# Attention block: MLA scores placed among v's products, value products among r's, weight splits for v and w_out on ScalarE and VectorE

## The chip, the cores and the metric

The kernel runs on one core of one Trainium2 chip. The metric is the device time of one execution in microseconds (us). The core has a tensor engine (PE for its products, PEld for its weight loads), a vector engine (DVE), a scalar engine (ACT), GpSimd (POOL) and SyncE (SP), whose queue issues nearly all transfers from HBM. Each engine works through its own instruction list in order. They wait for one another through semaphores.

## The reference, cut to what matters

The program computes two transformer blocks on 256 tokens of width 1024. The first block adds 16 meta tokens in front, projects the normed input `u` with `w_in`, runs a gated linear attention (GLA) and a latent softmax attention (MLA) side by side, joins them through `w_out`, and then runs a mixture of 64 experts. The second block (convolution and mLSTM mixers with feed-forward layers) follows and is not touched.

```python
z = u @ w_in                                   # q, k, v, r, a_low, q_lat, kv_lat, k_rope
y_gla = gla_group(q, k, v, r, a_low, ...)      # chunks of 64, 4 heads, gate silu(r) at the end
y_mla = mla_group(q_lat, kv_lat, k_rope, ...)  # scores, masked softmax, p @ v, 4 heads of 128
h = h + concat([y_gla, y_mla]) @ w_out
h = h + hier_moe(rmsnorm(h), ...)              # top 2 of 64 experts, 6.3 MB of weights each
```

All tensors are float32. Where the change works, weights and activations are split into a high part (fp32r, a rounded copy) and a low part (the rest), and a product is summed from three passes: high x high, high x low, low x high.

## The kernel before

`phase_a` holds the whole attention block. It streams `w_in` in 1 MB pieces and forms, in this order, the small latent projections (tiles `z`), q and k of GLA (`z` again), v (`v`, lines 671 to 680) and r (`r`, lines 690 to 707), and then the products with `w_out` (`wo`, lines 709 to 732). Every weight piece is split by `split` (line 1100): ACT writes the high part `wh`, and DVE, or POOL where the call has `gp` set, subtracts it from the raw piece and writes the low part `wl` (line 1120). The calls with `gp` are the first piece of the small projections, both pieces of v (line 675) and piece 3 of `w_out` (line 714). The tiles of high and low parts come from a pool of four buffers, so two pieces are alive at a time.

The order on PE is the order in which the Python code records it, with one addition. Side work is written as generators (`gates`, `keys`, `queries`, `values`, `gla`, `attend(b)` for the two blocks b of 128 queries). Each `yield` names a cost. A `unit` of main products advances a clock by its own cost and then `poll` runs every generator that has come due. So what a generator records lands on PE between two units. The other engines' lists are sorted by a scheduler that keeps the dependencies.

`attend(b)` forms the scores of four heads (tiles `qo`, `kn`, `qr_bd`, `kr`), takes the row maximum on DVE and the exponential on ACT into `pr`, transposes `pr` into `pT`, multiplies with the values `va` (the value products, line 508), divides by the sum, transposes again and splits the result into `yT`. `gla` does the same for the linear attention: transposes of `edl`, masked `attm`, the states `S`, the output products (`ps<-v,attm` and `ps<-S,q_bd`), the norm, the gate with `rg` and the split into `yT`.

At the start the input is normed: ACT and DVE form the row scale, DVE writes `x`, PE transposes it, ACT and DVE write the high and low parts `uT` (lines 290 to 312).

The weights of `w_out`, of the memory projection (`wkv`), the memory itself (`mem`) and the experts (`eg`, `eu`, `ed`, 1 MB pieces, six for each expert) go through a ring of buffers. SP issues a load when the buffer that it takes is free and the loads ahead of it in SP's list are issued. Seven more buffers appear where the attention's own tiles were (`a_done`, line 746), five more where `uT` and the split tiles were, after the last `wo` product. After `w_out` come the router (`route`, `router`), the gather of tokens and the experts.

Of the kernel before, what the change touches and what calls it, by code (L numbers as in the profile page):

```python
# [10 lines left out]
F32 = mybir.dt.float32  # L11
F32R = mybir.dt.float32r
# [77 lines left out]
class Kern:  # L90
# [150 lines left out]
    def phase_a(self):  # L241
# [71 lines left out]
        nc.gpsimd.memset(self.mv, 1.0)  # L313
# [144 lines left out]
        def y_tiles():  # L458
            if not yT:
                yT.extend(pw.tile([P, 2, KD, P], F32R, tag=f"uT{q}", name=f"yT{q}") for q in range(2))  # L460
            return yT

        def o_tile():
            if not late:
                late.append(self.mp.tile([P, 4, 4, P], F32, tag="xs", name="late"))
            return late[0]

# [5 lines left out]
        def attend(b, *needs):  # L473
            for c in needs:
                self.finish(c)
# [19 lines left out]
            yield 3.5  # L495
            pT = self.hl.tile([P, 2048], F32, tag="hl", name=f"pT{b}")[:, :1536].rearrange("p (j g t) -> p j g t", j=3, g=4)
            for j in range(2 + b):
                c0, n = toks[j]
                p = self.ps()
                pv = p.rearrange("p (a b) -> p a b", b=P)  # L500
                for g in range(4):
                    self.T(pv[:n, g, :], pp[:, g, c0:c0 + n])
                (nc.vector.tensor_copy if j != 1 else nc.scalar.copy)(pT[:n, j], pv[:n])
            yield 2.5
            ym = o_tile()[:, b]
            for g2 in range(2):
                p = self.ps()
                pv = p[:, :258].rearrange("p (a b) -> p a b", b=129)
                for gg in range(2):
                    for j in range(2 + b):  # L510
                        n = toks[j][1]
                        self.mm(pv[:, gg, :], pT[:n, j, 2 * g2 + gg, :], va[:n, j, 2 * g2 + gg, :],
                                start=j == 0, stop=j == 1 + b)
# [3 lines left out]
            yield 2.5  # L517
# [4 lines left out]
            self.split_t(*(t[:, b, 4:8] for t in y_tiles()), pv)  # L522

        def gla():
# [30 lines left out]
            yield 1.5  # L555
            self.finish(vc)
# [38 lines left out]
            for b in range(2):  # L595
                ov, o[b] = o[b], o_tile()[:, 2 + b]
                nc.vector.tensor_tensor(o[b], ov, self.bc(ri[:, b, :], [P, 4, P]), ALU.mult)
            past.append("o")
            yield 5.0
# [5 lines left out]
            for b in range(2):  # L605
# [6 lines left out]
                self.split_t(*(t[:, b, 0:4] for t in y_tiles()), yt)  # L612
# [61 lines left out]
        vf = [sb.tile([P, NT], F32, tag=f"rw{q}", name=f"vf{q}") for q in "oxtk"]  # L674
        for hf in range(2):
# [14 lines left out]
        self.finish(gt)  # L690
        attm = t4([P, 2, 4, P], "attm")
        kdt = sb.tile([NM, 2, P], F32, tag="qt", name="kdt")
        nc.gpsimd.memset(attm, 0.0)
        rp = [self.ps("r") for _ in range(2)]
        rdone = []
        ac = [None, None]
        vc = self.chain(values())
        oc = self.chain(gla())
        for hf in range(2):
            ws = self.split(rw[hf])  # L700
            for b in range(2):
                tpart(rp[b], ws, hf, 1 + b)
                if hf == 0:
                    ac[b] = self.chain(attend(b, kc, qc))
# [7 lines left out]
        for q, b in ((2, 0), (2, 1), (3, 0), (3, 1), (0, 0), (1, 0), (0, 1), (1, 1)):  # L712
            if q not in ws:
                ws[q] = self.split(wo[q], q == 3)
            self.wait(oc if q < 2 else ac[b])
            if not done:
                self.until(lambda: len(past) == 3)
# [4 lines left out]
            hi, lo = ws[q]  # L722

            def go():
                for nh in range(2):
                    cs = slice(nh * 512, nh * 512 + 512)
                    for k in range(2):
                        self.mm3(acc[b][nh], [t[:, b, 2 * q + k] for t in yT], (hi[:, k, cs], lo[:, k, cs]),
                                 q == 2 and k == 0, q == 1 and k == 1)
            self.unit(2.6, go)  # L730
# [5 lines left out]
    def load_memory(self):  # L736

        nc, mp = self.nc, self.mp
        mem = [mp.tile([P, 4 * NT], F32, tag="y", bufs=2, name=f"mem{b}")[:, :D] for b in range(2)]
# [24 lines left out]
    def route(self, b, acc):  # L764
# [8 lines left out]
        yield (1.4, 1.0)[b]  # L773
# [317 lines left out]
    def pair(self, ctx):  # L1091
# [5 lines left out]
        return pool  # L1097

# [807 lines left out]
```

## Time and profile before

| | |
|---|---|
| median of 3 runs | 2136.28 us (2135.34 to 2137.08) |
| profiled execution | 2137.44 us |
| its span, first to last instruction | 2135.7 us |
| mean granted TensorE clock | 0.983 of full |
| PE busy | 1979.5 us (93%) |
| DVE busy | 956.3 us (45%) |
| ACT busy | 665.1 us (31%) |
| POOL busy | 31.3 us (1%) |
| DMA | 605.14 MB, mean 283 GB/s |

The page's second part cuts the span in 40 slices of 53.4 us. The attention block fills the first three slices and part of the fourth (PE busy in tenths 8, 9, 8, 8; PEclk 9, 9, 7, 9; the DMA engines 6, 4, 4, 8). The experts fill the slices up to 21, with the DMA engines at 9 and 413 to 423 GB/s in nearly all of them. The second block fills the rest.

In a timeline row stand the start, the time that the row covers, the engine, the line, the operation, output<-inputs, the partitions x elements and the count, and in brackets the idle time of that engine just before and what ended it. A windows row gives the stretch, its length, the busy time and the count of instructions of PE, PEld, DVE, ACT and POOL, the granted clock (1.00 is 2.4 GHz, 0.50 is 1.2 GHz), the busy share of the DMA engines and GB/s.

### The profile page before, as it was taken

Reading aid. Unit: us, or ns where it says so; the run is one execution under the profiler, and the core shown is the slowest. Engines: PE = TensorE matmul, PEld = TensorE weight load, DVE = VectorE, ACT = ScalarE, POOL = GpSimd, SP = SyncE. Lnnn points to the kernel's source line nnn. Section 1 sums busy time; section 2 is a strip of 40 time slices with the busy share of each in tenths; the row PEclk is TensorE's granted clock in tenths of the full one; section 3 lists DMA queues with packets and bytes.
Section 4 is the critical chain, followed back from the end, with each engine's and each line's share of the span. In section 5 each row is a group of like instructions: output and inputs, shape, how many; then the busy total and the mean of one; then the engine's idle time right before and its main releaser. Section 6 shows DMA issues by size and latency. Waiting matters only on the chain.

```text
span 2135.7 us, 39455 instructions
## 1 busy us (share of the span) xinstructions
PE 1979.5 (93%) x17351; PEld 1454.0 (68%) x17351; DVE 956.3 (45%) x1452; ACT 665.1 (31%) x877; POOL 31.3 (1%) x28
## 2 busy tenths in 40 slices
PE   8989888888889888888889999999999999999998
PEld 7767454444445443544447998879998998888997
DVE  6553322222222222222227545775547445887545
ACT  6423111111111111111114433544434432854432
POOL 3000000000000000000000000000000000000000
PEclk9979999999999999999999999999999999999999
DMA  6448999999999999999995654546555553445551
GB/s 228 177 178 331 420 375 422 421 422 421 422 422 421 422 421 422 421 422 423 413 386 223 237 182 145 206 146 219 188 190 186 196 180 112 145 159 183 192 183 74
DMA packets 86001, 605.14 MB, mean 283 GB/s; under 512 B 9889, under 2 KB 10145, under 8 KB 14914
## 3 DMA queue, kind: packets, MB, share of 16 engines
q1 hardware_dynamic: 85602, 602.55, 71.2%
q8 instruction: 138, 2.26, 0.4%
q14 instruction: 37, 0.30, 0.0%
q10 hardware_dynamic: 224, 0.03, 0.0%
HBM read 601.49 MB, written 1.05 MB: 282 GB/s over the span
## 4 chain that ended last, share of the span: by engine, by line
PE 62%; DMA 28%; DVE 6%; ACT 2%; issue 1%; SPq 0%; DVEq 0%; ACTq 0%
DMA ed<-in_expert_w_down 14%; PE fu L118 11%; PE fd L118 11%; PE fg L118 11%; DMA eu<-in_expert_w_up 9%; DMA eg<-in_expert_w_gate 5%; PE ps L118 4%; PE pd L118 4%; PE po L118 4%; PE cu L118 3%; PE mu L118 2%; PE pg L118 2%; PE mo L118 2%; PE pu L118 2%; DVE wl L1120 1%
## 5 line engine op out<-in xcount | busy, mean ns | idle before, releaser
L973 DVE SCALAR_TENSOR_TENSOR h<-po,G,h 128x512 f32<-128x512 f32 x256 | 192.1, 751 | 354.4 <-PE po L118 334.1
L1120 DVE TENSOR_TENSOR wl<-wc,wh 128x2048 fp32r<-128x2048 f32 (+2 forms) x108 | 240.4, 2232 | 157.2 <-ACT wh L1114 157.1
L1114 ACT ACTIVATE wh<-wc 128x2048 fp32r<-128x2048 f32 (+2 forms) x114 | 213.3, 1872 | 261.3 <-issue 146.9
L118 PE MATMUL pd<-ed,hT 128*32 128x512 f32 x1024 | 244.8, 630 | 40.2 <-DMA ed<-in_expert_w_down 27.3
L118 PE MATMUL po<-y,C 128*128 128x512 f32 x512 | 236.7, 605 | 3.8 <-ACT C L967 3.8
L118 PE MATMUL fd<-wh,hT 128*128 128x512 f32 x704 | 225.5, 396 | 0.0
L118 PE MATMUL fg<-xT,wh 128*128 128x256 f32 x1152 | 203.8, 279 | 0.0
L118 PE MATMUL fu<-xT,wh 128*128 128x256 f32 x1152 | 203.6, 279 | 0.0
L118 PEld LDWEIGHTS po<-y,C 128*128 128x128 f32 x512 | 91.8, 189 | 144.6 <-ACT y L962 72.6
L118 PEld LDWEIGHTS fg<-xT,wh 128*128 128x128 f32 x1152 | 176.8, 188 | 1.7
L118 PEld LDWEIGHTS fu<-xT,wh 128*128 128x128 f32 x1152 | 175.4, 188 | 0.0
L1120 DVE TENSOR_TENSOR wl<-wr,wh 128x2048 fp32r<-128x2048 f32 x52 | 119.1, 2292 | 110.1 <-ACT wh L1114 110.1
L118 PE MATMUL pu<-eu,xg 128*32 128x128 f32 x4096 | 130.7, 274 | 38.2 <-DMA eu<-in_expert_w_up 35.8
L118 PE MATMUL fg<-xT,wl 128*128 128x256 f32 x576 | 160.8, 279 | 0.0
L118 PE MATMUL fu<-xT,wl 128*128 128x256 f32 x576 | 160.8, 279 | 0.0
L947 DVE TENSOR_TENSOR hg<-sg,pu 128x128 f32<-128x128 f32 x64 | 18.4, 288 | 305.3 <-PE pu L118 305.3
L118 PEld LDWEIGHTS fd<-wh,hT 128*128 128x128 f32 x704 | 132.1, 188 | 31.5
L118 PEld LDWEIGHTS pd<-ed,hT 128*32 128x32 f32 x1024 | 50.4, 112 | 142.8 <-issue 91.8
L118 PEld LDWEIGHTS pu<-eu,xg 128*32 128x32 f32 x4096 | 110.0, 110 | 52.0 <-DMA eu<-in_expert_w_up 41.7
L1114 ACT ACTIVATE wh<-wr 128x2048 fp32r<-128x2048 f32 x52 | 99.6, 1917 | 135.9 <-issue 58.5
L118 PE MATMUL fd<-wl,hT 128*128 128x512 f32 x352 | 138.5, 393 | 0.0
L118 PEld LDWEIGHTS pg<-eg,xg 128*32 128x32 f32 x4096 | 107.7, 110 | 44.6 <-issue 38.9
(507 smaller groups left out, 2517.1 us busy)
## 6 DMA issues: line engine op xcount, KB each, us to landing
eg<-in_expert_w_gate SPq DMA_DIRECT2D x128, 1024.0 KB, 19.7
eu<-in_expert_w_up SPq DMA_DIRECT2D x128, 1024.0 KB, 19.7
ed<-in_expert_w_down SPq DMA_DIRECT2D x128, 1024.0 KB, 19.7
wc<-in_ffn_w_gate SPq DMA_DIRECT2D x44, 1024.0 KB, 4.7
wc<-in_ffn_w_up SPq DMA_DIRECT2D x44, 1024.0 KB, 4.6
wr<-in_ffn_w_down SPq DMA_DIRECT2D x44, 1024.0 KB, 4.6
wc<-in_w_in_conv SPq DMA_DIRECT2D x10, 1024.0 KB, 4.7
wr<-in_w_out SPq DMA_DIRECT2D x8, 1024.0 KB, 4.8
```

The lines of the kernel that those rows point to most:

```text
L118: self.nc.tensor.matmul(out, lhsT, rhs, start=start, stop=stop, **kw)
L947: nc.vector.tensor_mul(hg, sg, pu[:, :P])
L973: nc.vector.scalar_tensor_tensor(self.h[:, b, cs], p, self.G[:, b, e:e + 1], self.h[:, b, cs], ALU.mult, ALU.add)
L1114: nc.scalar.activation(hi, raw, AF.Copy)
L1120: (nc.gpsimd if gp else nc.vector).tensor_sub(lo, raw, hi.bitcast(F32))
```

## The change

Nothing is added to or taken from the arithmetic. Eight things differ.

1. `attend` no longer forces its inputs to be complete; it yields until they are. Both `attend` generators and `gla` are started inside v's loop, so the scores stand between v's products of the second half.
2. `attend` waits until both blocks have their scores, then transposes and forms the value products in smaller steps. `r`'s products are recorded in units of one k tile (cost 0.65) and no longer of four (2.6), so the pieces stand between them.
3. Tiles: the transposed probabilities lie in tiles of the block's own pool and, for the 16 meta tokens, in `mv`; the divided result lies in `mk`; MLA's split result has its own tiles `yM` (tag `y`), and `yT` holds GLA's half alone. `mv` is set to one later, by `load_memory`.
4. v, r and `w_out` are split by a new function `split2`: two halves, high part on ACT, low part on DVE, none on POOL.
5. `w_out`'s units are halved, and pieces 0 and 1 (GLA's) are taken together for each half of the columns. The ring grows (`a_done`) once the value products and GLA's output are recorded.
6. `kdt` has a tile of its own.
7. `route` of block 1 yields 0.4 and no longer 1.0.
8. The set-to-one of `mv` at the program's start is gone, so POOL's list begins with `kra`.

```diff
-        nc.gpsimd.memset(self.mv, 1.0)
...
+        def y_mla():
+            if not yM:
+                yM.extend(self.mp.tile([P, 4 * NT], F32R, tag="y", bufs=2, name=f"yM{q}")[:, :1024].rearrange(
+                    "p (b k t) -> p b k t", b=2, k=4) for q in range(2))
+            return yM
...
         def attend(b, *needs):
             for c in needs:
-                self.finish(c)
+                while not c.done:
+                    yield 0.5
...
-            yield 3.5
-            pT = self.hl.tile([P, 2048], F32, tag="hl", name=f"pT{b}")[:, :1536].rearrange("p (j g t) -> p j g t", j=3, g=4)
+            yield 3.0
+            while len(past) < 2:
+                yield 0.5
+            px = t4([P, 1 + b, 4, P], f"pT{b}")
+            pT = [pm[:, b]] + [px[:, j] for j in range(1 + b)]
...
-            yield 1.5
-            self.finish(vc)
+            while not (vc and vc[0].done and len(past) >= 2):
+                yield 0.5
...
-            def go():
-                for k in range(4):
-                    x = [t[:, 4 * hf + k, c0:c0 + n] for t in uT]
-                    self.mm3(dst[:n, :], x, (hi[:, k, :], lo[:, k, :]), hf == 0 and k == 0, hf == 1 and k == 3)
-            self.unit(2.6, go)
+            for k in range(4):
+                x = [t[:, 4 * hf + k, c0:c0 + n] for t in uT]
+                self.unit(0.65, lambda: self.mm3(dst[:n, :], x, (hi[:, k, :], lo[:, k, :]), hf == 0 and k == 0, hf == 1 and k == 3))
...
         for hf in range(2):
-            ws = self.split(vw[hf], True)
+            ws = self.split2(vw[hf])
             for f in range(4):
                 zpart(vp[f][:, :NT], ws, hf, f * P, P, 0)
                 if hf == 1:
                     nc.scalar.copy(vf[f], vp[f][:, :NT])
+                elif f < 2:
+                    ac[f] = self.chain(attend(f, kc, qc))
+                elif f == 2:
+                    oc = self.chain(gla())
...
-        for q, b in ((2, 0), (2, 1), (3, 0), (3, 1), (0, 0), (1, 0), (0, 1), (1, 1)):
-            if q not in ws:
-                ws[q] = self.split(wo[q], q == 3)
-            self.wait(oc if q < 2 else ac[b])
+        for group, b in (((2,), 0), ((2,), 1), ((3,), 0), ((3,), 1), ((0, 1), 0), ((0, 1), 1)):
+            for q in group:
+                if q not in ws:
+                    ws[q] = self.split2(wo[q])
+                self.wait(oc if q < 2 else ac[b])
             if not done:
-                self.until(lambda: len(past) == 3)
+                self.until(lambda: len(past) == 5)
...
+    def split2(self, raw):
+
+        self.n += 1
+        k, n = raw.shape[1:]
+        hi, lo = (self.hl.tile([P, 2048], F32R, tag="hl", name=f"w{q}{self.n}")[:, :k * n].rearrange("p (k n) -> p k n", n=n)
+                  for q in "hl")
+        for u in range(2):
+            ks = slice(u * k // 2, (u + 1) * k // 2)
+            self.nc.scalar.activation(hi[:, ks], raw[:, ks], AF.Copy)
+            self.nc.vector.tensor_sub(lo[:, ks], raw[:, ks], hi[:, ks].bitcast(F32))
+        return hi, lo
```

On PE, the value products (`ps<-va,...`) stood in one piece behind the transposes of `pr` (names: `pT` the transposed probabilities, `late` the result tile).

```order
L115 MATMUL ps_1019<-cst_63,pr_232 16x128 x4
L115 MATMUL ps_1025<-cst_63,pr_232 128x128 x4
L115 MATMUL ps_1031<-cst_63,pr_232 128x128 x4
L118 MATMUL ps_1039<-va,pT_1005 128x129 x4
L118 MATMUL ps_1047<-va,pT_1005 128x129 x4
L118 MATMUL ps_1055<-va,pT_1018 128x129 x6
L118 MATMUL ps_1065<-va,pT_1018 128x129 x6
L115 MATMUL ps_1075<-cst_63,late 128x128 x4
```

Now the first of them stand between products of r's second half.

```order
L118 MATMUL r_840<-wh_951,uT_120 128x512
L118 MATMUL r_840<-wl_952,uT_120 128x512
L118 MATMUL r_840<-wh_951,uT_121 128x512
L118 MATMUL ps_963<-va,mv 128x129
L118 MATMUL ps_963<-va,pT_881 128x129
L118 MATMUL ps_963<-va,mv 128x129
L118 MATMUL ps_963<-va,pT_881 128x129
L118 MATMUL r_840<-wh_951,uT_120 128x512
L118 MATMUL r_840<-wl_952,uT_120 128x512
L118 MATMUL r_840<-wh_951,uT_121 128x512
```

Twelve r products (four units) now follow the last value product, where before nothing of r was left.

On ACT, the end of r and the start of `w_out` before (`yT` both halves of the split result, `wh_1161` piece 3 of `w_out`):

```order
L503 COPY pT_1005<-ps_1012 128x512
L491 ACTIVATE pr_232<-ps_996,mx_999 64x208
L491 ACTIVATE pr_232<-ps_996,mx_999 64x272
L503 COPY pT_1018<-ps_1025 128x512
L1114 ACTIVATE wh_1161<-wo_942 128x2048
L1132 ACTIVATE yT_1081<-rg 128x512
L1132 ACTIVATE yT_1081<-ps_1093 128x512
```

And now (`wh_1172` is piece 3, in the buffer of r's second piece; `yM` MLA's split result; L721 the gate silu(r)):

```order
L608 ACTIVATE rg<-ps_985 128x512
L608 ACTIVATE rg<-ps_1001 128x512
L721 ACT_TABLE_LOAD
L721 ACTIVATE rg<-r_840 128x512
L1125 ACTIVATE wh_1172<-wo_1083 128x1024
L1162 ACTIVATE yM_1071<-ps_1066 128x512
L721 ACTIVATE rg<-r_841 128x512
L1125 ACTIVATE wh_1172<-wo_1083 128x1024
L1162 ACTIVATE yM_1071<-ps_1125 128x512
```

A half of piece 3 now stands ahead of each part of `yM` that the first `wo` products read.

At the program's start the scheduler also put one ACT instruction elsewhere. Before (`wh_239` is the high part of the first small projection, whose low part is POOL's; `uT` the transposed input):

```order
L304 ACTIVATE gx<-gx,ur_129 16x1024
L1132 ACTIVATE uT_120<-ps_172 128x4x128
L1132 ACTIVATE uT_120<-ps_179 128x4x128
L1132 ACTIVATE uT_120<-ps_186 128x4x16
L1132 ACTIVATE uT_120<-ps_193 128x4x16
L1114 ACTIVATE wh_239<-win_100 128x1856
L1132 ACTIVATE uT_120<-ps_200 128x4x128
```

And now:

```order
L304 ACTIVATE gx<-gx,ur_129 16x1024
L1144 ACTIVATE wh_238<-win_100 128x1856
L1162 ACTIVATE uT_120<-ps_172 128x4x128
L1162 ACTIVATE uT_120<-ps_179 128x4x128
L1162 ACTIVATE uT_120<-ps_186 128x4x16
L1162 ACTIVATE uT_120<-ps_193 128x4x16
L1162 ACTIVATE uT_120<-ps_200 128x4x128
```

The weight copy moved from behind four `uT` copies to ahead of all of them.

## Rows read from the trace of the kernel before

**Rows 1.** The page's part 4, the chain that ended last, by engine.

```profile
PE 62%; DMA 28%; DVE 6%; ACT 2%; issue 1%; SPq 0%; DVEq 0%; ACTq 0%
```

**Rows 2.** Windows just before the first expert and through the experts.

```profile
176.00:180.00 4.00, 4.00 (x73) 3.98 (x76) 0.29 (x2) 3.04 (x8) 0.00 (x0) 1.00 0.01 4
...
300.00:1100.00 800.00, 700.93 (x8477) 363.31 (x8475) 201.42 (x338) 120.97 (x263) 0.00 (x0) 0.98 1.01 420
```

**Rows 3.** Timeline of SP and PE: a load behind w_out, the first expert.

```profile
160.45 0.33 SPq L141 DMA_DIRECT2D ed<-in_expert_w_down  x1
...
178.74 1.96 PE L118 MATMUL pg<-eg,xg 128*32 128x128 f32 x64
```

**Rows 4.** Windows of the attention block, cut where PE waits or its clock changes.

```profile
53.35:57.79 4.44, 0.21 (x1) 0.00 (x0) 4.36 (x4) 0.42 (x2) 3.22 (x1) 0.83 0.78 258
57.79:63.03 5.24, 5.24 (x19) 4.83 (x20) 2.42 (x6) 0.85 (x3) 0.00 (x0) 0.50 0.46 181
...
76.12:108.70 32.58, 32.24 (x183) 24.76 (x181) 20.61 (x49) 18.94 (x29) 0.00 (x0) 1.00 0.45 175
108.70:110.76 2.06, 0.00 (x1) 0.00 (x0) 1.83 (x11) 1.21 (x3) 0.00 (x0) 1.00 0.61 207
110.76:112.73 1.97, 1.97 (x10) 1.64 (x10) 1.23 (x5) 0.59 (x1) 0.00 (x0) 0.53 1.02 412
112.73:125.92 13.19, 13.19 (x41) 9.80 (x41) 4.59 (x11) 1.91 (x1) 0.00 (x0) 0.50 0.58 225
125.92:129.06 3.14, 2.46 (x13) 2.22 (x12) 2.21 (x5) 1.27 (x3) 2.71 (x1) 0.68 0.00 0
129.06:132.09 3.03, 0.73 (x3) 0.30 (x3) 3.03 (x3) 0.47 (x1) 1.83 (x1) 0.88 0.00 0
132.09:138.26 6.17, 5.49 (x14) 4.01 (x14) 0.56 (x2) 0.60 (x1) 0.00 (x0) 0.51 0.75 275
...
149.95:151.16 1.21, 0.00 (x1) 0.00 (x0) 1.16 (x1) 0.00 (x0) 0.00 (x0) 1.00 0.02 7
```

**Rows 5.** Timeline of POOL and DVE where both subtract.

```profile
46.57 2.89 DVE L532 TENSOR_TENSOR edl<-zk,edl 128x544 f32<-128x544 f32 x1 [2.11 <-ACT zk L656]
...
52.07 4.50 POOL L1120 TENSOR_TENSOR wl<-win,wh 128x2048 fp32r<-128x2048 f32 x1 [2.30 <-ACT wh L1114]
...
52.25 5.03 DVE L448 TENSOR_TENSOR qr_bd<-qx,qt 64x256 f32<-64x256 f32 x2
...
59.85 0.85 DVE L448 TENSOR_TENSOR qr_bd<-qx,qt 64x256 f32<-64x256 f32 x2
...
128.56 2.88 DVE L1133 TENSOR_TENSOR yT<-rg,yT 128x512 fp32r<-128x512 f32 x1
```

**Rows 6.** Timeline of the program's start: POOL, DVE, SP, ACT, PE.

```profile
4.83 2.34 POOL L290 TENSOR_TENSOR gx<-met,gx 16x1024 f32<-16x1024 f32 x1
...
5.18 1.99 DVE L163 SCALAR_TENSOR_TENSOR u2nt<-ur,um 16x1 f32<-16x1 f32 x1
...
10.28 0.33 SPq L761 DMA_DIRECT2D br<-in_br  x1
...
13.63 1.74 ACT L1114 ACTIVATE wh<-win 128x1856 fp32r<-128x1856 f32 x1
...
15.91 5.35 PE L118 MATMUL z<-uT,wh 128*80 128x272 f32 x32 [0.54 <-ACT uT L1132]
```

**Rows 7.** Timeline of ACT and DVE: prices of steps around w_out.

```profile
100.23 1.28 ACT L491 ACT_TABLE_LOAD   x1 [0.72 <-DVE mx L488]
...
131.36 0.68 DVE L1133 TENSOR_TENSOR yT<-ps,yT 128x512 fp32r<-128x512 f32 x1
...
137.61 0.60 ACT L1132 ACTIVATE yT<-ps 128x512 fp32r<-128x512 f32 x1 [8.08 <-PE ps L115]
...
141.37 1.92 ACT L1114 ACTIVATE wh<-wo 128x2048 fp32r<-128x2048 f32 x1 [3.16 <-PE wo L118]
...
143.32 2.29 DVE L1120 TENSOR_TENSOR wl<-wo,wh 128x2048 fp32r<-128x2048 f32 x1 [4.39 <-ACT wh L1114]
```

More of the change, by code (lines that the diff above doesn't have):

```diff
@@ L456, in phase_a, with y_gla @@
         yT = []
-        def y_tiles():
+        yM = []
+        def y_mla():
[3 more added lines that the diff above has]
+            return yM
+        def y_gla():
             if not yT:
-                yT.extend(pw.tile([P, 2, KD, P], F32R, tag=f"uT{q}", name=f"yT{q}") for q in range(2))
+                yT.extend(pw.tile([P, 2, 4, P], F32R, tag=f"uT{q}", name=f"yT{q}") for q in range(2))
             return yT
@@ L464, in o_tile @@
             if not late:
-                late.append(self.mp.tile([P, 4, 4, P], F32, tag="xs", name="late"))
+                late.append(self.mp.tile([P, 2, 4, P], F32, tag="xs", name="late"))
             return late[0]
+        pm = self.mv.rearrange("p l m h d -> p (l m h d)")[:NM, :1024].rearrange("p (b g t) -> p b g t", b=2, g=4)
+        yo = self.mk.rearrange("p b j m -> p b (j m)").rearrange("p b (g t) -> p b g t", t=P)
         def r_tile():
@@ L502, in attend @@
                     self.T(pv[:n, g, :], pp[:, g, c0:c0 + n])
-                (nc.vector.tensor_copy if j != 1 else nc.scalar.copy)(pT[:n, j], pv[:n])
-            yield 2.5
-            ym = o_tile()[:, b]
+                (nc.vector.tensor_copy if j != 1 else nc.scalar.copy)(pT[j], pv[:n])
+                yield 0.5
+            yield 1.5
+            ym = yo[:, b]
             for g2 in range(2):
@@ L516, in attend @@
                 nc.vector.tensor_tensor(ym[:, 2 * g2:2 * g2 + 2, :], pv[:, :, 0:P], rc.to_broadcast([P, 2, P]), ALU.mult)
-            yield 2.5
+                yield 0.5
+            past.append(f"v{b}")
+            yield 2.0
             p = self.ps()
@@ L521, in attend @@
                 self.T(pv[:, g, :], ym[:, g, :])
-            self.split_t(*(t[:, b, 4:8] for t in y_tiles()), pv)
+            self.split_t(*(t[:, b] for t in y_mla()), pv)
         def gla():
@@ L611, in gla @@
                 nc.vector.tensor_tensor(yt, pv, self.bc(self.col("gla"), [P, 4, P]), ALU.mult)
-                self.split_t(*(t[:, b, 0:4] for t in y_tiles()), yt)
+                self.split_t(*(t[:, b] for t in y_gla()), yt)
         groups = (("kra", 384, 80, 0), ("kv", 256, 128, 0), ("l0", 0, 128, NM), ("l1", 128, 128, NM))
@@ L674, in phase_a @@
         vf = [sb.tile([P, NT], F32, tag=f"rw{q}", name=f"vf{q}") for q in "oxtk"]
+        vc, rdone, ac = [], [], [None, None]
+        self.finish(gt)
+        attm = t4([P, 2, 4, P], "attm")
+        kdt = sb.tile([NM, 2, P], F32, name="kdt")
+        nc.gpsimd.memset(attm, 0.0)
         for hf in range(2):
-            ws = self.split(vw[hf], True)
+            ws = self.split2(vw[hf])
             for f in range(4):
@@ L689, in values @@
                 yield 0.5
[L690 to L693, printed above, removed]
+        vc.append(self.chain(values()))
         rp = [self.ps("r") for _ in range(2)]
[L695 to L698, printed above, removed]
         for hf in range(2):
-            ws = self.split(rw[hf])
+            ws = self.split2(rw[hf])
             for b in range(2):
                 tpart(rp[b], ws, hf, 1 + b)
-                if hf == 0:
-                    ac[b] = self.chain(attend(b, kc, qc))
         for b in range(2):
@@ L721, in phase_a, with go @@
                 acc[b] = [self.ps("wo") for _ in range(2)]
[L722 to L730, printed above, removed]
+            def go(q, nh):
+                hi, lo = ws[q]
+                cs = slice(nh * 512, nh * 512 + 512)
+                for k in range(2):
+                    x = [t[:, b, 2 * q + k] for t in y_gla()] if q < 2 else [t[:, b, 2 * q + k - 4] for t in y_mla()]
+                    self.mm3(acc[b][nh], x, (hi[:, k, cs], lo[:, k, cs]), q == 2 and k == 0, q == 1 and k == 1)
+            for nh in range(2):
+                for q in group:
+                    self.unit(1.3, lambda: go(q, nh))
             if q == 1:
```

10 lines of the change are left out of this document (6 added, 4 removed).

## The prediction

> **What bounds the kernel now.** I read the chain first, then the windows around the hand-over to the experts, then the attention block's windows, and only then single instructions. The chain [rows 1] is PE for 62% and DMA for 28%. The DMA part is the experts' stage: between 300 and 1100 us the DMA engines are fully busy at 420 GB/s [rows 2], and its bytes are fixed. A faster attention block cannot shorten that stage; it can only let it begin earlier. So the question is what starts it. Just before the first expert product at 178.74 [rows 3] the DMA engines stand still (share 0.01 from 176 to 180 [rows 2]): all buffers of the ring are full, and the next load waits until the first expert has used one. The loads before that wait for the attention block too: the load at 160.45 [rows 3] takes a buffer that the last `wo` product frees. Both hand-overs are released by PE, so time that PE gains before 160 us should move the whole experts' stage, one for one.
>
> Within the attention block the reader is to look at two columns of rows 4, PE busy and the clock. PE loses time there in two ways. It stands still: 4.23 us of 4.44 up to 57.79, 0.34 in the long stretch up to 108.70, then 2.06, 0.68, 2.30, 0.68 and 1.21. And it runs at 1.2 GHz instead of 2.4 after the first wait (5.24 us) and, with one short break, from 110.76 to 138.26. The rest of the block runs at full clock without gaps.
>
> **The change part by part.** v's split first. A subtraction on POOL takes 4.50 us, and a DVE instruction with two SBUF inputs that meets it takes until POOL's end: a pair of `qr_bd` additions took 5.03 us beside 0.85 for the same pair later, and `edl` took 2.89 [rows 5]. The first of these holds back the query rows on PE, which is the wait of 4.23; the low clock follows it (5.24 us at 0.50, so 2.62 us lost). *The Trainium skill, "SBUF — State Buffer", section "Who interferes with whom", says that a DVE instruction with two SBUF inputs and a GpSimd instruction that reads SBUF exclude one another for the whole instruction, whoever starts first. These rows agree; what it says against this change stands under the rivals.* With `split2` DVE gets 2 x 2.29 = 4.58 us of subtractions [rows 7]. The first has the 2.11 us in which DVE waited ahead of `edl` [rows 5], and the stalls that go are 2.2 and 4.2 us, so DVE comes out ahead and the wait goes. Gain: 4.23 + 2.62 = 6.85 us. If DVE's part did not fit, at most 2.3 of it would come back as a wait.
>
> Scores and value products. Their products are the same in number. Moved among v's and r's, they have company: 32 us of such work ran at full clock with 0.34 idle [rows 4], and r's last four units stand after the last value product. What goes is the wait of 2.06 for the last exponentials, which are now followed by most of r before their value products stand in line; the half-clock transposes (1.97 us at 0.53, 0.93 lost); the value products at 0.50 (13.19 us, 6.60 lost); the transposes behind them (3.14 us at 0.68, 1.00 lost); and the 0.34. Sum 10.93. ACT changes its table between exponentials and the gate once instead of four times (1.28 us each [rows 7]), all hidden beside PE.
>
> `w_out`. POOL's piece goes, and with it the `yT` subtraction of 2.88 us [rows 5] (0.68 without POOL [rows 7]); so the waits of 0.68, 2.30 and 0.68 and the low clock on 5.49 us of products (2.70 lost at 0.51) go, as does the 1.21 that the last piece's low part caused [rows 4]. Sum 7.57.
>
> New waits. The pool of four split buffers now ties piece 3 of `w_out` to r's last product: ACT's first half of it (0.96, half of 1.92) starts there and stands ahead of `yM` (0.60) [rows 7], and four transposes of the result (some 0.4) are all that PE has meanwhile, so PE waits 0.96 + 0.60 + an estimated 0.2 of hand-over - 0.4 = 1.3 us. DVE then does half a low part (1.15, half of 2.29) and the low `yM` (0.68) from the end of that first half, 0.27 later than two products (0.46) and the wait cover, with hand-overs 0.7 us. Pieces 0 and 1 are next: piece 1's buffers are those of piece 3, so its split starts when piece 3's products end, and six products of piece 0 cover it only in part (1.4 us; ten such products and four transposes took 5.49 at half clock [rows 4]): 0.96 + 1.15 to the first low half, less the 1.4 and the first high product, some 0.5 short, and 0.6 at the second half. Together 1.3 + 0.7 + 1.1 = 3.1 us; none before in this form, so I bound it by 1.2 and 5.0, the shortest and the two longest waits of rows 4 that are of this kind (1.21; 2.30 + 2.06 + 0.68).
>
> The start. Without the setting of `mv` (0.96 us, the first thing that POOL did) POOL's `gx` (4.83, 2.34 long) and the DVE instruction that it blocks (5.18, 1.99 instead of 0.2 [rows 6]) come 0.96 earlier, and the row scales after them. The weight copy of 1.74 us now runs from the landing of its piece, which is when the `br` load could be issued, 10.28 [rows 6], to 12.0, so ahead of the last `uT` copies and no longer between them. I follow it: four `uT` copies from 12.0 to 13.5, the next to 14.1, its low part on DVE at 15.1; the `z` products start at about 14.2 and wait 0.4 once, so 1.4 us before 15.91. Bounds: gain 1.8, loss 3.6 (below).
>
> The end of the block. From the load at 160.45 to the first expert product 18.3 us pass [rows 3]. `route` yields 0.6 less, and fewer transposes stand ahead of it, some 0.8 us; against it the exponential of the router now needs a table load (1.28 [rows 7]), hidden if it runs in ACT's pause of 1.4 before it. Taken at 0.4 lost, between -0.8 and 1.3. `mem` is loaded behind the last use of `yM`, some 13 us before the end of `wo`; its two transfers and the 2 MB queued ahead of it take 7 us at 420 GB/s, so they are there in time.
>
> Sum: 6.85 + 10.93 + 7.57 + 1.4 - 3.1 - 0.4 = 23.25 us. The profiled execution took 2137.44 and would take 2114.2; the median is 1.16 lower, so 2113.
>
> **The rivals.** (1) The start collides. POOL's subtraction now starts at 12.0, right behind DVE's last small scale steps, which end at about 11.4. If these come 0.7 us later than I think, one of them waits for POOL (some 4.2 us), and `x`, its transposes and `z` wait with it. For it: the 1.99 us of rows 6 is just such a block. Against it: the 0.96 gained ahead of it is plain. Price 1.4 + 3.6 = 5.0: 2118. *By the skill's rule of the SBUF page cited above, an exclusion for the whole instruction, this would happen to any two-input DVE step that falls in that stretch; no row of this trace has that meeting with these steps.*
>
> (2) The clock falls once more. Falls followed waits of 4.2 us, of 2.06, and of 0.68 + 2.30 close together; 1.21 was followed by none [rows 4]. The new waits of 1.3 and 0.7 close together lie between. A low stretch of some 6 us (rows 4 have 5.24 and 6.17) costs half, 3.1; one among the value products as well, where 15.2 us stayed low before, costs up to 7.5 more. So 2116 to 2124; I take 2118. *The Trainium skill, "TensorE: Matmul & The Clock Gate", section "A second HAM failure mode: psum-queue depth-cycling", tells of a PE whose clock swings because it pauses often between groups that cycle through PSUM, and the new order has many small groups between r's products. By it this rival would be the likely one; against it the 32.58 us of mixed small groups before 108.70 held 1.00 [rows 4].*
>
> (3) The experts' stage doesn't move: the stream of weights turns out to be late instead of the products, since eight 1 MB loads and `mem` now fall into fewer us. From the end of piece 3's products to the first expert there are, by the sum above, some 13 + 18 us, and 8.4 MB need 20 at 420 GB/s. Price: up to all of it, 2136, no change.
>
> (4) Slower: the clock falls early in the interleaved stretch and stays at 1.2 GHz, because small groups never bring it back, as 13.19 us of value products did not [rows 4]. Every us of work done at half clock costs one, so it decides from 23 us of work. The mixed stretch of 32.58 us and the 6.6 of the value products are 39 us: 2113 + 39 = 2152. For it: the value products' row. Against it: r's and v's dense products stand between, and dense `v` products brought the clock back within 5.24 us.
>
> **How the numbers follow.** Chances: forecast 0.62, with its own range 2108 to 2117 (new waits 1.2 to 5.0, start 1.8 gain or nil, end -0.8 to 1.3); rival 1 0.10; rival 2 0.16; rival 3 0.06; rival 4 0.04; the rest, a gain above 28 us or waits that I missed, 0.02. A measurement of this kernel tells about 0.2% (4.3 us) from no change. Forecast and rivals 1 and 2 are faster by more: 0.62 + 0.10 + 0.16 + 0.01 = 0.89. No change: rival 3, 0.06, and 0.01 of the rest. Slower: 0.04. The range that holds 8 in 10 takes in the forecast's and rivals 1 and 2 up to 2124: 2107 to 2124.
>
> **What would show it.** In the profile after: `z` starting near 14.5; no PE wait ahead of `v` and the clock at 1.00 there; the value products in about half of 13.2 us; two waits, of about 1.3 and 0.7, at the first `wo` products, ended by ACT and DVE; the first expert product near 155.5; the experts' stage as long as before. The prediction is wrong if the first expert comes early and the end doesn't, if the clock row shows 0.5 in the interleaved stretch, or if waits that ACT or DVE end add up to more than 5 us between `v` and the end of `wo`.

## The result, and the profile after

| | before | after |
|---|---|---|
| median of the runs | 2135.81 us (4 runs) | 2113.08 us (4 runs, 2112.87 to 2115.72) |
| profiled execution | 2137.44 us | 2113.02 us |
| span | 2135.7 us | 2111.2 us |
| PE busy | 1979.5 us | 1968.1 us |
| POOL busy | 31.3 us | 17.5 us |

The ratio is 0.9895, with a 95% interval of 0.988 to 0.9909. The forecast was 2113.0 us.

The chain that ended last, by engine, of the changed kernel, stands against [rows 1] (its shares on the page don't add up to 100%, and no reading below rests on it):

```profile
PE 50%; DMA 31%; DVE 4%; ACT 1%; issue 1%; SPq 0%; DVEq 0%; ACTq 0%
```

The windows of the changed kernel show the attention block in larger pieces than [rows 4], since little is left to cut at, and the experts' stage as in [rows 2]:

```profile
14.00:57.00 43.00, 43.00 (x289) 39.27 (x288) 27.38 (x54) 27.55 (x50) 5.53 (x5) 1.00 0.56 215
57.00:70.00 13.00, 13.00 (x85) 11.47 (x84) 7.61 (x16) 5.67 (x11) 0.00 (x0) 1.00 0.54 202
70.00:108.00 38.00, 38.00 (x226) 29.38 (x225) 23.23 (x64) 15.85 (x28) 0.97 (x1) 1.00 0.50 181
108.00:112.00 4.00, 2.38 (x13) 1.55 (x12) 3.38 (x5) 2.53 (x4) 0.00 (x0) 1.00 1.02 428
112.00:124.00 12.00, 12.00 (x59) 9.87 (x57) 6.17 (x9) 5.14 (x7) 0.00 (x0) 1.00 0.58 218
124.00:136.00 12.00, 11.24 (x54) 8.87 (x52) 9.04 (x21) 0.93 (x2) 0.00 (x0) 1.00 0.80 293
...
300.00:1100.00 800.00, 701.69 (x8441) 362.72 (x8440) 198.92 (x336) 121.60 (x265) 0.00 (x0) 0.97 1.01 418
```

From 14 to 108 us PE has no gap, and the clock is 1.00 throughout. The experts' stage runs at the same 1.01 DMA share. What moved is its beginning, and by the same amount the end. The timeline of SP and PE (compare [rows 3]):

```profile
136.02 0.33 SPq L141 DMA_DIRECT2D ed<-in_expert_w_down  x1
...
154.29 1.95 PE L118 MATMUL pg<-eg,xg 128*32 128x128 f32 x64
```

The first expert product is 24.45 us earlier, the execution 24.42. PE's timeline has four waits left between the first `z` product and the experts, all at `w_out`:

```profile
109.16 0.50 PE L118 MATMUL wo<-wh,yM 128*128 128x512 f32 x1 [0.96 <-ACT yM L1162]
...
110.53 0.73 PE L118 MATMUL wo<-wh,yM 128*128 128x512 f32 x2 [0.65 <-DVE yM L1163]
...
124.96 0.50 PE L118 MATMUL wo<-wl,yT 128*128 128x512 f32 x1 [0.58 <-DVE wl L1126]
...
126.09 0.50 PE L118 MATMUL wo<-wl,yT 128*128 128x512 f32 x1 [0.17 <-DVE wl L1126]
```

On DVE the two steps of [rows 5] that POOL held are back at their own length (2.89 and 5.03 before), and the start of `z` has come forward (15.91 in [rows 6]):

```profile
44.86 0.72 DVE L550 TENSOR_TENSOR edl<-zk,edl 128x544 f32<-128x544 f32 x1
...
48.20 0.85 DVE L447 TENSOR_TENSOR qr_bd<-qx,qt 64x256 f32<-64x256 f32 x2
...
14.29 2.10 PE L118 MATMUL z<-uT,wh 128*80 128x272 f32 x8
```

### The profile page after: what moved, and what is told of

Same layout as the page of the kernel before. It is cut to its first block, busy times and chain, and to the rows that moved or that the text cites. A ratio compares the mean times of both kernels' runs of the same rounds, so it can differ in the third digit from the quotient of the medians.

```text
span 2111.2 us, 39473 instructions
## 1 busy us (share of the span) xinstructions
PE 1968.1 (93%) x17351; PEld 1444.6 (68%) x17351; DVE 952.3 (45%) x1463; ACT 662.2 (31%) x883; POOL 17.5 (1%) x25
## 4 chain that ended last, share of the span: by engine, by line
PE 50%; DMA 31%; DVE 4%; ACT 1%; issue 1%; SPq 0%; DVEq 0%; ACTq 0%
DMA ed<-in_expert_w_down 12%; DMA eu<-in_expert_w_up 12%; PE fu L118 11%; PE fd L118 11%; PE fg L118 11%; DMA eg<-in_expert_w_gate 7%; PE pd L118 3%; PE cu L118 3%; PE mu L118 2%; PE po L118 2%; PE mo L118 2%; PE ps L118 1%; PE pg L118 1%; PE pu L118 1%; DVE wl L1150 1%
```

## The experiments

"First expert" below is the start of the first `pg` product, which the trace gives to 0.01 us. Whole executions of one kernel differ by more than some of the effects looked for. The kernel before took between 2127.6 and 2140.6 us in its 28 executions beside these experiments. Five of them, all on one occasion, took 2127.6 to 2129.1, and the seven others of that occasion 2134.9 to 2140.6. None of the five was profiled. The step of about 8 us fits the 8.5 that the half clock costs from 110.76 to 129.06 in [rows 4]. So this half clock is likely not in every execution of the kernel before: the change gains some 15 us beside those five and 22.7 beside the median of 2135.81.

**v's split alone, in the kernel before.**

```diff
-            ws = self.split(vw[hf], True)
+            ws = self.split2(vw[hf])
```

> The kernel before, with one edit: both pieces of v are split in two halves on ScalarE and VectorE, none on GpSimd. My theory (GpSimd's subtraction holds VectorE's two-input additions, and the 4.23 us wait and the 5.24 us at half clock come from that): the first v product near 51.9 instead of 58.45, no wait ahead of it, clock 1.00 behind it, the first expert product near 171.9, 2129.4 us. Rival (VectorE becomes the bound, its own 4.58 us are late): 2.3 us come back as a wait in front of v, 2131.7. Rival (a later wait takes up the gain, since the exponentials and w_out's splits set when things happen): the first expert stays near 178.7, 2136.

Measured: 2125.79 us (2122.07 to 2129.21, 4 runs), ratio 0.9953 (0.9937 to 0.997). In the profiled execution, the fastest of the four, the first `v` product is at 53.08, 5.37 us earlier, and has no wait ahead of it:

```profile
53.08 1.35 PE L118 MATMUL v<-uT,wh 128*128 128x272 f32 x8
```

With the half of 4.58 us that ran at low clock behind it before, that is 7.7 us for 6.85 expected. The first expert is at 164.39, 14.35 us earlier. The rest comes from a place that the edit doesn't touch. Windows of that run, from the wait for the last exponentials through the value products to `w_out`:

```profile
101.18:103.23 2.05, 0.00 (x1) 0.01 (x1) 1.83 (x10) 1.20 (x3) 0.00 (x0) 1.00 0.62 134
103.23:114.30 11.07, 10.02 (x61) 7.78 (x61) 7.76 (x21) 3.66 (x5) 2.23 (x1) 1.00 0.88 356
114.30:123.22 8.92, 6.15 (x16) 4.31 (x16) 4.05 (x3) 0.47 (x1) 2.30 (x1) 0.62 0.43 150
```

The wait of 2.05 is there as before, but here the clock held behind it. In [rows 4] the same products ran at 0.50 behind the same wait. So a wait of that length does not by itself decide the clock. It fell later in this execution, behind waits of 1.06 and 2.77 at `w_out` (the 0.62 of the last row). That the clock fell earlier in the slower executions would fit their times, but only the fastest was profiled.

**w_out's splits alone, in the kernel before.**

```diff
-                ws[q] = self.split(wo[q], q == 3)
+                ws[q] = self.split2(wo[q])
```

> The kernel before, with one edit: all four pieces of w_out are split in halves on ScalarE and VectorE, none on GpSimd. My theory (term w_out of the sum): the waits of 0.68, 2.30, 0.68 and 1.21 go and the clock is full behind them: 7.57 us less, first expert near 171.2, 2128.7. Rival (the low clock there is carried over from the value products before it and is not the waits' doing): only the waits go, 4.9 us, first expert near 173.9, 2131.4. Rival (VectorE's 2.3 us for the low part of that piece push the yT subtractions back): half of it, 2 to 3 us less, 2134.

Measured: 2129.66 us (2127.8 to 2131.7), ratio 0.9969 (0.9957 to 0.9982). The first expert is at 173.72, 5.02 us earlier. The waits of 2.30 and 1.21 are gone; the two of 0.69 in front of `yT`'s first use remain. Windows, from the transposes of the probabilities on:

```profile
111.15:112.20 1.05, 1.05 (x9) 0.91 (x9) 1.02 (x4) 0.25 (x1) 0.00 (x0) 1.00 1.04 421
112.23:128.20 15.97, 15.96 (x53) 12.15 (x52) 7.21 (x17) 2.31 (x3) 0.00 (x0) 0.50 0.56 217
128.87:132.70 3.83, 3.83 (x9) 3.01 (x10) 3.01 (x4) 0.99 (x2) 0.00 (x0) 0.50 0.28 47
132.70:155.00 22.30, 21.61 (x99) 17.45 (x99) 12.17 (x24) 5.68 (x6) 0.00 (x0) 1.00 0.60 228
```

From the first `w_out` product (129.06 before, 128.87 here) to the first expert the edit is worth 4.83 us: the rival's 4.9, and not 7.57. In this execution the half clock of the value products runs on into the first `w_out` products for 3.83 us. In the kernel before it did not. There the clock was back before the first `w_out` product, and it fell again behind the wait of 2.30 ([rows 4], from 132.09):

```profile
127.00:128.00 1.00, 1.00 (x7) 1.00 (x7) 0.98 (x3) 0.26 (x1) 1.00 (x1) 0.54 0.00 0
128.00:131.00 3.00, 1.11 (x6) 0.44 (x4) 3.00 (x3) 1.49 (x3) 2.89 (x1) 1.00 0.00 0
```

So the low clock of `w_out` in the kernel before was a fall of its own behind the waits, as my sum has it. Without the waits the value products' half clock can still reach that far.

**v's low parts back on GpSimd, in the changed kernel.**

```diff
-            ws = self.split2(vw[hf])
+            ws = self.split(vw[hf], True)
```

> The changed kernel, with v's two pieces split as before (low part on GpSimd). My theory: the wait of 4.2 us ahead of v and 2.6 us of low clock come back, first v product near 58.7, first expert near 161.1, 2119.9 us. Rival (it was not the split but the waits that attend no longer forces, or the new place of the scores, that took the wait away): at most 1 us more than the changed kernel, 2114. Rival (worse than before, since scores and their maxima now fall into the same stretch as the second GpSimd subtraction): 4 us more on top, 2124.

Measured: 2120.14 us (2119.34 to 2122.51, 4 runs), first expert 160.75, 6.46 us later. Windows around the returned wait, and the two instructions that make it:

```profile
51.50:55.74 4.24, 0.01 (x1) 0.00 (x0) 4.16 (x4) 0.42 (x2) 3.02 (x1) 0.75 0.77 259
55.74:60.45 4.71, 4.71 (x17) 4.30 (x18) 2.42 (x6) 0.50 (x2) 0.00 (x0) 0.50 0.55 212
60.45:79.91 19.46, 19.46 (x126) 16.77 (x125) 9.99 (x24) 9.14 (x19) 0.00 (x0) 1.00 0.30 109
```

```profile
50.02 4.50 POOL L1150 TENSOR_TENSOR wl<-win,wh 128x2048 fp32r<-128x2048 f32 x1 [2.28 <-ACT wh L1144]
...
50.21 5.01 DVE L447 TENSOR_TENSOR qr_bd<-qx,qt 64x256 f32<-64x256 f32 x2
```

4.24 of wait and half of 4.71 are 6.6, against 6.85 in the sum. The yields in `attend` and the new order have no part in this term.

**The value products behind r.** In the changed kernel:

```diff
             yield 3.0
-            while len(past) < 2:
+            while not rdone:
                 yield 0.5
```

> The changed kernel, with one condition: the transposes of the probabilities and the value products wait until r is done, so they stand in one piece behind r's products, as in the kernel before, but with the exponentials long finished. My theory (a wait, and then a piece of nothing but small products, brings the half clock): a wait of 1 to 2 us before the value products for the copies of the transposed probabilities, the value products at 0.50 clock in about 13 us, and w_out behind them at low clock in part: first expert near 154.3 + 8 to 11, 2121 to 2124 us. Rival (the fall came from the wait of 2.06 us for the exponentials alone, and the place in the order is worth nothing): clock stays at 1.00, the value products take 7.4 us, first expert at most 2 us later, 2114 to 2115.

Measured: 2113.6 us (2113.43 to 2113.95, 4 runs), first expert 154.52. The rival was right and my theory fell: next to nothing is lost (0.23 us at the first expert). One window covers all from r's end to the first `w_out` product:

```profile
97.90:110.13 12.23, 11.30 (x73) 8.77 (x71) 9.21 (x22) 5.25 (x8) 0.96 (x1) 1.00 0.29 95
```

**Scores among r's products again, value products behind r.** The edit above, and `attend` started in r's loop:

```diff
-                elif f < 2:
-                    ac[f] = self.chain(attend(f, kc, qc))
...
                 tpart(rp[b], ws, hf, 1 + b)
+                if hf == 0:
+                    ac[b] = self.chain(attend(b, kc, qc))
```

> The changed kernel with the scores back among r's products and the value products in one piece behind r, as in the kernel before; the splits, tiles and w_out's units stay new. Theory as it stands after the run in which only the value products were moved behind r and nothing was lost: the place of the value products is worth nothing, what costs is a wait of PE for the last exponentials. By it the wait of about 2 us ahead of the transposes of the probabilities comes back, and behind it the clock is at 0.50 in some executions and 1.00 in others (the wait of 2.05 us was followed by 1.00 in the kernel before with v's split alone changed): 2115.5 us where the clock holds, up to 2124 where the value products run at half clock, so executions some 8 us apart. Rival (the scores' place is worth nothing either, since r's units of one k tile and the smaller steps of attend cover the exponentials): no wait over 0.5 us, 2113 to 2114, executions within 1 us.

Measured: six executions, 2110.92, 2110.99 and 2111.09 us with a mean clock of 0.989 to 0.99, and 2115.81, 2116.21 and 2116.24 with 0.983 to 0.986. The expected wait did not come back. The last scores stand far ahead of the transposes of the probabilities here, and right in front of them in the kernel before, where the wait of 2.06 followed. This run, then the kernel before:

```profile
83.53 0.62 PE L118 MATMUL ps<-kr,qr_bd 128*128 128x272 f32 x2
...
97.51 2.35 PE L115 MATMUL ps<-cst,pr 128*16 128x128 f32 x20
```

```profile
106.88 0.62 PE L118 MATMUL ps<-kr,qr_bd 128*128 128x272 f32 x2
107.34 1.36 PE L115 MATMUL ps<-cst,pr 128*16 128x128 f32 x11
110.76 2.03 PE L115 MATMUL ps<-cst,pr 128*16 128x128 f32 x9 [2.06 <-ACT pr L491]
```

Both times the scores are started in r's loop. Among what differs are r's units of one k tile, between which the scores can be recorded four times as often. That these units drew the scores forward is likely, but was not tried by itself.

Yet the clock fell. The profiled execution is one of the three longer ones; its windows, and PE at the moment of the fall:

```profile
91.32:104.30 12.98, 12.98 (x92) 9.12 (x91) 8.02 (x22) 6.11 (x8) 0.00 (x0) 1.00 0.74 287
104.30:114.60 10.30, 9.55 (x31) 7.24 (x32) 4.49 (x13) 0.60 (x1) 0.96 (x1) 0.50 0.36 126
114.60:127.00 12.40, 12.40 (x60) 10.09 (x58) 6.08 (x8) 5.51 (x7) 0.00 (x0) 1.00 0.68 245
```

```profile
103.13 0.48 PE L118 MATMUL ps<-va,mv 16*128 16x129 f32 x2
103.54 0.71 PE L118 MATMUL ps<-va,pT 128*128 128x129 f32 x4
104.18 0.73 PE L118 MATMUL ps<-va,mv 16*128 16x129 f32 x2
```

PE shows no gap in the 12.98 us before, and the same pair of products goes from 0.48 to 0.73 us. The 10.30 us at 0.50, with 9.55 busy, cost some 4.8, close to the 5.1 between the two groups of executions. So both of my theories on the clock fall in part: no wait that the trace shows is needed. What PE had done since r's last product was nothing but small float32 products: the GLA output, the transposes and the value products.

**The same, with the GLA output among r's products.**

```diff
-            while not (vc and vc[0].done and len(past) >= 2):
+            while not (vc and vc[0].done):
```

> The run with the scores late, with one more condition taken away: the linear attention no longer waits for both blocks' scores, so its output products stand among r's and five of r's units come between them and the transposes of the probabilities. In the run before this one PE had no gap from r's end at 91.3 to 111 and did nothing but small float32 products there, and the clock fell at about 104, 13 us into that stretch, in three of six executions (2116.2 beside 2111.0). Theory now (it is the unbroken stretch of small products, not a wait, that brings the half clock): the stretch behind r is some 12 us, as in the run with only the value products late, the clock stays at 1.00 and all executions lie within 1 us at about 2111 to 2112. Rival (small products late in the block bring it whatever stands between): executions 5 us apart again. Rival (a wait): with only five units between the last scores and the transposes the exponentials are late, a wait of 1 to 2 us, and 2113.

Measured: 2113.23 us (2112.17 to 2114.69, 4 runs), first expert 154.35. The stretch behind r, in the profiled execution:

```profile
98.40:110.67 12.27, 11.49 (x74) 8.79 (x72) 9.84 (x22) 7.04 (x10) 0.96 (x1) 1.00 0.14 40
```

The two groups, 5 us apart, are gone, which speaks for the theory, but weakly: if half of the executions fell as before, four without a fall would still come about once in 16 times. The executions lie 2.5 us apart and not 1, and the time is not the 2111 of the run before, so the saving that I expected with it was not there.

**A longer wait at w_out.** The first `yM` copy is done twice:

```diff
+            if b == 0:
+                for _ in range(1):
+                    nc.scalar.activation(y_mla()[0][:, b], pv, AF.Copy)
             self.split_t(*(t[:, b] for t in y_mla()), pv)
```

> The changed kernel with the high part of the first yM written twice, so the first w_out product waits for ScalarE longer: 0.96 becomes about 2.0 us (0.60 for the second copy and 0.60 for the gate's activation that comes between), with the wait of 0.65 behind it. Theory (a wait of this length ahead of dense products can bring half clock): about 1.1 us from the wait itself, and in some executions some 6 us at 0.50 behind it, so 3 us more: 2114.2 in the executions without, 2117 with. Rival (only waits of 4 us or a wait beside small products bring it): 2114.2 in all, executions within 1 us.

Measured: 2115.35 us (2112.26 to 2117.22, 6 runs), executions 5 us apart. The profiled one (2116.67):

```profile
107.95:109.89 1.94, 0.01 (x2) 0.01 (x1) 1.48 (x2) 1.94 (x5) 0.00 (x0) 1.00 1.02 427
109.89:111.13 1.24, 0.97 (x3) 0.53 (x4) 1.24 (x3) 0.89 (x1) 0.00 (x0) 1.00 1.03 436
111.13:114.71 3.58, 3.58 (x12) 2.84 (x12) 1.52 (x2) 0.60 (x1) 0.00 (x0) 0.53 0.78 323
```

Behind 1.94 and 0.27 us of waiting (0.96 and 0.65 in the changed kernel) the clock fell, for 3.58 us, and came back among `w_out`'s products. That is 1.7 us lost where my second rival took 3.1. The six times are spread out and don't fall into two groups.

**VectorE's scale steps meet GpSimd.**

```diff
-        for j in range(3):
+        for j in range(5 if name == "u1" else 3):
```

> The changed kernel with two more Newton steps on the row scale of the second block of tokens (four small VectorE instructions with two SBUF inputs, about 0.45 us for each step), so the last of them fall into GpSimd's subtraction, which starts at 11.81. The mechanism of my first rival (such a VectorE instruction is held until GpSimd's instruction ends): one step takes until about 15.9, x, its transposes and the first z product come some 4.5 us later, near 18.8, first expert near 158.8, 2117.6 us. Other theory (steps of one element in each partition are too short to be held, or GpSimd is held in their place): only the 0.9 us of the steps, z near 15.2, first expert near 155.2, 2114.

Measured: 2118.5 us (2116.25 to 2120.43, 5 runs), first `z` 19.16, first expert 159.27, 4.98 us later. POOL's and DVE's timelines:

```profile
11.96 4.11 POOL L1150 TENSOR_TENSOR wl<-win,wh 128x1856 fp32r<-128x1856 f32 x1 [5.71 <-ACT wh L1144]
```

```profile
11.57 0.16 DVE L167 SCALAR_TENSOR_TENSOR ur<-u1nt,ur 128x1 f32<-128x1 f32 x1
...
12.02 4.06 DVE L167 SCALAR_TENSOR_TENSOR ur<-u1nt,ur 128x1 f32<-128x1 f32 x1
```

A step on one element per partition that takes 0.16 us takes 4.06 when it starts 0.06 us behind POOL's subtraction. My first rival is a real mechanism; in the changed kernel these steps end at 11.43, 0.38 us ahead of POOL's start at 11.81.

**mv set first.** The setting is put back at the start and stays in `load_memory` too:

```diff
+        nc.gpsimd.memset(self.mv, 1.0)
         nc.gpsimd.memset(kra, 1.0)
```

> The changed kernel with the setting of mv put back as the first thing that GpSimd does. By the term for the start: GpSimd's gx product and the VectorE step that it holds come 0.95 us later, the weight copy of 1.75 us falls among the uT copies again, the first z product near 15.9 instead of 14.3, the first expert product near 155.9, 2114.7 us. Rival (the start's gain came from elsewhere, the shorter list of memory waits): z stays within 0.3 us of 14.3.

Measured, one execution: first expert 156.16, 2116.34 us, and `z` where it was in [rows 6], behind the same wait:

```profile
15.91 5.43 PE L118 MATMUL z<-uT,wh 128*80 128x272 f32 x32 [0.54 <-ACT uT L1163]
```

The start's gain is this edit's.

**No subtraction on GpSimd at all.**

```diff
-        rest = [self.split(t, u == 0) for u, t in enumerate(rest)]
+        rest = [self.split(t) for u, t in enumerate(rest)]
```

> The changed kernel with the last low part that GpSimd formed (the first weight piece, 4.14 us at 11.81) formed by VectorE (2.1 us). If VectorE's order leaves it behind the uT low parts: it ends near 18, the z products that use it stand behind some 5 us of others, so no wait over 0.5 us and the first expert product within 0.5 us of 154.3, 2113. Rival: VectorE takes it ahead of the uT low parts, z waits for them, up to 2 us more, 2115.

Measured, one execution: `z` at 14.71, first expert 154.40, 2113.85 us. Nothing is gained, but the collision above can't happen in it.

**Without the waits at w_out.** Two edits to the changed kernel, and the version that the experiments point to:

```diff
             past.append(f"v{b}")
-            yield 2.0
+            yield 0.5
...
         nc.scalar.activation(self.xs[:, b, :], h, AF.Copy, scale=r)
+        if b == 0:
+            ex = self.rp.tile([P, 1], F32, name="ex")
+            nc.scalar.activation(ex, r, AF.Exp)
```

> The changed kernel with two edits. The yield behind the last value product is 0.5 and no longer 2.0, so the transposes of the divided result stand between r's last products and ScalarE writes the first yM before it splits piece 3 of w_out. And an exponential of one column right behind the first xs makes ScalarE load the exponential's table in its idle time and not in the router's chain (1.28 us there). Theory: the waits of 0.96 and 0.65 at the first w_out products go (1.6 us) and the router's chain is 1.3 shorter: first expert near 151.4, 2110.2 us. Rivals: the transposes among r's last products wait for the divided result and give the 1.6 back (152.9, 2111.8); the table load is loaded again or holds up the copies of the memory behind it (1.3 not gained, 152.7, 2111.5).

Measured: 2112.38 us (2110.78 to 2113.38, 6 runs), first expert 152.48, 1.81 us earlier. The waits of 0.96 and 0.65 are gone. The table load is out of the router's chain and gave nothing. ACT in this run, then in the changed kernel:

```profile
141.27 0.22 ACT L842 ACTIVATE ge<-ge 128x16 f32<-128x16 f32 x1 [0.34 <-DVE ge L841]
143.70 0.22 ACT L865 ACTIVATE ee<-ee 128x16 f32<-128x16 f32 x1 [2.22 <-DVE ee L864]
```

```profile
143.07 1.28 ACT L839 ACT_TABLE_LOAD   x1 [0.33 <-DVE ge L838]
144.37 0.22 ACT L839 ACTIVATE ge<-ge 128x16 f32<-128x16 f32 x1
145.55 0.22 ACT L862 ACTIVATE ee<-ee 128x16 f32<-128x16 f32 x1 [0.97 <-DVE ee L861]
```

Both times the second exponential waits for DVE, whose own steps between the two had hidden the load. The first expert's 1.81 us are the two waits and 0.2 more. Little of them reaches the median (0.7 us lower, on another occasion than the changed kernel's runs, so not told apart from it): the first product of the second block comes 1.29 us earlier, and in the profiled execution the clock is 0.97 from 1080 to 1200 us, where it was 1.00.

## Why the prediction held, and where it did not

The time was right, and so was the frame: the attention block's gain moved the experts' stage one for one. That the forecast of 2113.0 was met to 0.1 us is luck. By PE's marks the gain was 1.2 us more than the sum, and the 1.16 by which the median was taken to lie under the profiled execution was not there after the change. By PE's own marks, the forecast's terms against what the trace shows:

| stretch on PE | forecast | measured |
|---|---|---|
| to the first `z` | -1.4 | -1.62 |
| first `z` to first `v` | -4.56 | -4.98 |
| first `v` to first `wo` | -12.6 | -13.30 |
| first `wo` to the router's products | -5.1 | -4.53 |
| router's products to first expert | +0.4 | -0.02 |
| sum | -23.25 | -24.45 |

The second row is the wait of 4.23 and the 0.33 of low clock that lie ahead of the first `v`; the third is the other 2.29 of low clock, 10.93 and the old wait of 0.68, less the new wait of 1.3; the fourth is the rest of `w_out`'s 7.57 less 1.8. Eight transposes of GLA's result, 0.8 us, moved from the third row into the fourth, which the sum did not count. The forecast's lower bound of 2108 is not what its three terms give: 0.4 at the start, 1.9 of waits and 1.2 at the end are 3.5 us, so 2109.5.

*v's split*: right, by itself (the run with GpSimd put back, 6.46 for 6.85).

*Scores and value products*: the size was right, and much of the reason was not. The 2.06 and the half clock are gone, as I said. The mixing itself costs little: PE needs 56.35 busy us from the first `v` to the first `wo` product, and the same products would have needed 55.9 before at full clock (70.61, less 3.09 of waits, 10.8 of low clock and the 0.8 of the eight transposes). But I took the new places of the scores and of the value products as the cure. With both put back behind their old neighbours the wait of 2.06 did not return, so something that stayed in that run removed it, most likely r's finer units. And I counted the half clock as following from the wait, as something certain. It can come without a wait that the trace shows, it doesn't always come behind one, and with the value products in one piece behind r it stayed away too. Some executions of the kernel before, about 8 us shorter, seem not to have had it. What the new order does is to leave no long run of small products behind r, and no wait there. Which of the two was decisive in the kernel before stays open: its fall at 110.76 stands behind both, 10 us of small products since r's last and then 2.06 of wait.

*w_out*: right. The fourth row gained 4.53 with 1.40 of new waits and the 0.8 of transposes in it, so 6.7 beside the 6.89 counted there. Alone, in the kernel before, the splits gave only 4.83: one wait of 0.69 stayed, and the value products' half clock reached into `w_out` in that execution. The new waits are 2.36 where I had 3.1: the low part of piece 1 is 0.75 late and not 1.1. A slip stands in the second wait: the low `yM` comes 0.57 late by the figures given (1.15 + 0.68, less 0.60 + 0.2 + 0.46) and not 0.27; the 0.7 made of it with hand-overs was close all the same, 0.65.

*The start*: right, and so near the collision as to be luck in part. I took a margin of 0.7 us, and it is 0.38.

*The end of the block*: the table load does stand in the chain, where I had hoped to see it hidden in ACT's pause, and costs nothing all the same, because DVE has steps of its own beside it. The 0.8 us that I counted as gained there did not show either: the stretch is 0.02 shorter.

The rivals: the collision and the clock's fall at `w_out` did not happen in the profiled execution, but both exist, a short step away. That one of the four executions of the changed kernel took 2115.72 would fit such a fall; it was not profiled. The third rival is out, since first expert and end moved by the same 24.4 us. So is the fourth, with a clock of 1.00 from 14 to 108. Part of its reason was a misreading of [rows 4]: in the kernel before, the clock came back at 128, while PE had run nothing but transposes and value products since 110.76.

## What to carry to other kernels

Before a subtraction goes to GpSimd, look what steps with two inputs in SBUF VectorE has in that stretch: the price is up to the whole of GpSimd's instruction (4.06 of 4.11 us here), on whatever waits for VectorE. Read a fall of the clock as a risk with a price, not as a fixed part of the time, and compare whole executions beside the profiled one before giving it to a cause. In front of a stage that the DMA engines bound, mark its first product in each trace: it tells effects of 1 us in that execution that the spread of whole executions hides.

## What the runs showed of the hardware

- The clock can fall with no wait of PE to be seen: 1.00 to 0.50 at 104.3, after 12.98 us of small float32 products without a gap, in the profiled one of six executions, three of which took 2111.0 us and three 2116.1. The Trainium skill, "TensorE: Matmul & The Clock Gate", section "A second HAM failure mode: psum-queue depth-cycling", puts such swings down to frequent short idling between groups; the windows row shows PE busy for the whole 12.98 us. The ends of products are modelled in it, so idling too short to show is not excluded.
- A VectorE step of 0.16 us on one column waits out GpSimd's 4.1 us as a long one does. The Trainium skill, "SBUF — State Buffer", section "Who interferes with whom", says so of any instruction with two SBUF inputs, and the trace agrees. A step with one of its two inputs in PSUM was not held: `x`, whose `gm` lies there, kept 0.7 us for each of its two in the changed kernel, the second of them inside GpSimd's subtraction from 11.81 to 15.95:

```profile
11.47 1.40 DVE L303 SCALAR_TENSOR_TENSOR x<-h,ur,gm 128x512 f32<-128x512 f32 x2
```

- The clock came back while PE was at work, and not only on large products: after 3.83 us of `w_out`'s in one run, 3.58 in another, 4.71 of query and `v` products behind the wait of 4.24, and in the kernel before at 128, among transposes that followed the value products.
